# Gate arithmetic and sums of x queued behind the latest weight split, in a fused mLSTM and attention layer

## The chip, the cores and the metric

The kernel runs on one core of a Trainium2 chip. The metric is the device time of one execution in microseconds (us). Five engines work side by side, each with its own queue of instructions: TensorE (PE in the profile; PEld is its loading of weights), VectorE (DVE), ScalarE (ACT), GpSimd (POOL) and SyncE (SP), which here only starts DMA transfers. An engine takes its instructions strictly in the order of its queue: one that waits holds up all behind it.

## The reference

One layer of a decoder is computed for a prompt of 512 tokens and for 8 x 4 sample tokens, 544 tokens together, in float32. What matters here:

```python
u = jnp.einsum('btd,dc->btc', x, w_in)                  # 2048 -> 18952 columns
# q_m, k_m, v_m, o_m, z_m, q_a, k_a, v_a, z_a, g_m, g_a, i_pre, f_pre
ig = i_pre + b_igate                                    # 4 heads: "the gates"
lf = log_sigmoid(f_pre + b_fgate)
b = cumsum(lf)                                          # per chunk, then running maxima, exp: decay factors of the mLSTM
h_m = mlstm(q_m, k_m, v_m, ig, lf);  h_a = sliding_window_attention(q_a, k_a, v_a)
y = sigmoid(g_m) * (branch_m @ w_proj_m) + sigmoid(g_a) * (branch_a @ w_proj_a)
out = layernorm(alpha * x + y @ w_out)
```

The keys and values of the attention (k_a, v_a) and the last state are outputs too.

## The kernel before

**Precision.** Each float32 operand is split into a high part (a rounding copy on ACT) and a low part (the difference, on DVE). `split` (L196 to L202) does it for a block of weights of 128 x 1024: `A.copy(wh)` at L200 and `V.tensor_tensor(wl)` at L201; `hilo` (L239) does it for activations. A product is three matmuls: high x high, high x low, low x high.

**Stage 1, plain products.** x is transposed on TensorE and split (L287 to L310). Then `gemm` computes two blocks of attention values (VA_, L536) and two of keys (KA, L546), each in two halves of the 2048 rows, with TensorE's results in a pair of PSUM banks, of which there are two buffers (`mm`, L216). Beside these there are four small PSUM buffers of one bank (`sm`, L118). Within the second value product stand the matmuls of the gates (`gates_half`, L325 to L343), whose results lie in a third `mm` tile, `gates_ps`.

**Stage 2, pairs.** Pairs of weight blocks are computed from seven half products in place of eight (`paired`, L645). They need sums of quarters of x: `x_sums` (L496) makes `s1`, `n2` and `n3`, `last_sum` (L515) makes `s4`. Before half product number n of a pair `prepare` (L585) forms a sum of weights (L592) and splits it; that is written three half products ahead and has a raised priority (`AHEAD = 400`). `wh` and `wl` have two buffers each, so a split waits until TensorE is done with the half product two before its own. `half_product` (L604) issues 16 matmuls with the high weights (L612) and 8 with the low ones (L614). `gather` (L616) collects results. The first three pairs are the merge gates: at their end `end_gates` (L1163) puts a sigmoid on both results.

**What sets the order.** The text is traced first. A scheduler with a model of the engines' times then orders each engine's queue: of the instructions that are ready it takes the one with the best priority (the place in the text, less what `high_priority` grants), so work can move far ahead of its place. `tc.issue_after(ins)` ties what is traced under it to a place behind `ins` on the same engine; it is an order, not a wait for the end of `ins`. In stage 2 TensorE's queue alone keeps the order of the text (L1216).

**Side work** is written as generators. `spawn` (L136) puts one into the list `live`; `tick` (L141) lets each run to its next `yield`. `products` calls `tick` four times in each plain product of stage 1 (`every=4`), `paired` once after each half product. The generators here are `attn_values` (L466) and `attn_keys` (L482), which turn values and keys to rows with transposes on TensorE; `x_sums`; `gates` (L345), which computes the decay factors in rows of 4 x 544 in several stages and ends with transposes on TensorE (L448 to L462); `attentions` (L794), which waits until the gates have ended; and `samples`. Before, `drain` (L552) runs all generators of stage 1 to their end ahead of stage 2, and the first stage of `gates` is written just ahead of the pairs (L1211).

Of the kernel before, what the change touches and what calls it, by code (L numbers as in the profile page):

```python
# [23 lines left out]
NTS = 4  # L24
# [55 lines left out]
def _build(tc, nc, i, o, es):  # L80
# [43 lines left out]
    def r32(ap):  # L124
        return ap.bitcast(F32)

    def two(ap):
        return ap.rearrange("p (a b) -> p a b", a=2)
# [7 lines left out]
    def spawn(g):  # L136
        live.append(g)
# [8 lines left out]
    def drain():  # L146
        while live:
            tick()
# [47 lines left out]
    def split(raw, p=None, tags=("wh", "wl")):  # L196
        p = p or wp
        wh = p.tile([128, 8, 128], F32R, tag=tags[0], name=nm("wh"))
        wl = p.tile([128, 8, 128], F32R, tag=tags[1], name=nm("wl"))
        A.copy(wh[:], raw[:])  # L200
        V.tensor_tensor(out=wl[:], in0=raw[:], in1=r32(wh[:]), op=ALU.subtract)  # L201
        return wh, wl  # L202

    def products(ps, half, wh, wl, xh, xl, cols, every=8):
        for kk in range(8):
# [10 lines left out]
    def mm():  # L216
        return psA["mm"].tile([128, 2, 512], F32, tag="mm", name=nm("mm"))
# [107 lines left out]
    def gates_half(ps, half):  # L325
        raw = wr.tile([128, 8, 128], F32, tag="raw", name=nm("graw"))
        nc.sync.dma_start(raw[:, :, 0:8], win[:, half * 8:half * 8 + 8, GI:GI + 8])
        wa = wp.tile([128, 8, 128], F32R, tag="wh", name=nm("wga"))
        wb = wp.tile([128, 8, 128], F32R, tag="wl", name=nm("wgb"))
        G.memset(r32(wa[:]), 0.0)  # L330
        G.memset(r32(wb[:]), 0.0)
        for g in range(2):
            src = raw[:, :, g * 4:g * 4 + 4]
            hi = wa[:, :, g * 32:g * 32 + 4]
            A.copy(hi, src)
            A.copy(wb[:, :, g * 32:g * 32 + 4], src)
            V.tensor_tensor(out=wa[:, :, 64 + g * 32:68 + g * 32], in0=src, in1=r32(hi), op=ALU.subtract)
        for kk in range(8):
            k = half * 8 + kk
            for n, (a, b) in enumerate(((wa, xh), (wb, xl))):  # L340
                for f, c, w in EVEN:
                    PE.matmul(ps[:, f, :w], a[:, kk], b(k, c, w),
                              start=(k == 0 and n == 0), stop=(k == 15 and n == 1))  # L343

    def gates(ps):  # L345
# [7 lines left out]
            return ap.unsqueeze(2).to_broadcast([4, NB, NTS])  # L353

        ig, fg, u, u2 = row(), row(), row(), row()
        A.copy(two(u), ps[64:68, :, :272])
        A.copy(two(u2), ps[96:100, :, :272])
        V.scalar_tensor_tensor(two(ig), ps[0:4, :, :272], bi[:, 0:1], two(u), op0=ALU.add, op1=ALU.add)
        V.scalar_tensor_tensor(two(fg), ps[32:36, :, :272], 0.0, two(u2), op0=ALU.add, op1=ALU.add)
        V.tensor_scalar(fg, fg, bi[:, 1:2], None, op0=ALU.add)  # L360
        yield
        e_ = row()
        A.activation(e_, fg, AF.Abs)
        A.activation(e_, e_, AF.Exp, scale=-1.0)
# [101 lines left out]
    def attn_values(kk, vt):  # L466

        yield
        yield
        pt, pt2 = sm(), sm()  # L470
        for b in range(4):
            PE.transpose(pt[:, b * 128:b * 128 + 128], vt[:, b * 128:b * 128 + 128], ident)
        PE.transpose(pt2[:32, 0:128], vt[:, SEQ:T], ident)
        cs = slice(kk * 128, kk * 128 + 128)
        vr, vs = ev(512), ev(128)
        A.copy(vr[:], pt[:])
        V.tensor_copy(vs[:32], pt2[:32, 0:128])
        nc.sync.dma_start(d_vr[0:SEQ, cs].rearrange("(b p) c -> p b c", p=128), blk(vr[:]))
        nc.sync.dma_start(d_vr[SEQ:T, cs], vs[:32])
        nc.sync.dma_start(vb_p[0].rearrange("t k d -> t (k d)")[:, cs], vr[:, 384:512])  # L480
# [15 lines left out]
    def x_sums():  # L496

        for ch in range(4):
            ks_ = slice(ch * 2, ch * 2 + 2)
            r11, r21, r22 = (tx.tile([128, 2, HT], F32, tag="tx", name=nm("tx")) for _ in range(3))  # L500
            G.tensor_tensor(out=r21[:], in0=r32(a21[0][:, ks_]), in1=r32(a21[1][:, ks_]), op=ALU.add)
            k0 = (ch * 2) % 4
            h22, l22 = (r32(xk2[p][ch // 2][:, k0:k0 + 2, HT:T]) for p in range(2))
            V.tensor_tensor(out=r22[:], in0=h22, in1=l22, op=ALU.add)
            G.tensor_tensor(out=r11[:], in0=r32(a11[0][:, ks_]), in1=r32(a11[1][:, ks_]), op=ALU.add)
            V.tensor_tensor(out=r22[:], in0=r22[:], in1=r21[:], op=ALU.subtract)
            hilo(r22[:], s1[0][:, ks_], s1[1][:, ks_])
            yield
            V.scalar_tensor_tensor(r21[:], r11[:], -1.0, r21[:], op0=ALU.mult, op1=ALU.subtract)
            hilo(r21[:], n3[0][:, ks_], n3[1][:, ks_])  # L510
            V.tensor_tensor(out=r11[:], in0=r11[:], in1=r22[:], op=ALU.subtract)
            hilo(r11[:], n2[0][:, ks_], n2[1][:, ks_])
            yield
# [22 lines left out]
    for kk in range(2):  # L536
        ps = gemm(win, VA_ + kk * 128, xh, xl, raws=((raw0[0], raw0[1]), (raw0[2], None))[kk], every=4, prio=150 * kk,
                  before=gates_between if kk else None)
        if kk == 0:
            spawn(x_sums())  # L540
            gates_ps = mm()
        vt = ev()
        with ahead_of_sums():
            A.copy(two(vt[:]), pv(ps))
        spawn(attn_values(kk, vt))
    for kk in range(2):  # L546
        ps = gemm(win, KA + kk * 128, xh, xl, every=4, prio=150)
        kt = ev()
        with ahead_of_sums():
            A.copy(two(kt[:]), pv(ps))  # L550
        spawn(attn_keys(kk, kt))
    drain()  # L552
    for src, dst in ((d_ks, kb_s), (d_vr[SEQ:T], vb_s)):
        nc.sync.dma_start(dst[:, 124:128].rearrange("b t k d -> b t (k d)"), src.rearrange("(b t) c -> b t c", t=NTS))
    nc.sync.dma_start(kb_s[:, 0:124], i["state_attn_k"][:, NTS:128])
    nc.sync.dma_start(vb_s[:, 0:124], i["state_attn_v"][:, NTS:128])

# [236 lines left out]
    def attentions():  # L794
        while gates_ in live:
            yield
        for _ in last:
            pass
        esG.close()
        sp["pz"] = pool(esQ, "pz", 1)  # L800
        open_attention()
        state["open"] = True
        for k in range(16):
            if k % 4 == 0:
                kv = kv_head(k // 4)
            while k not in waiting:
                yield
            for _ in range(2 if k % 4 else 4):
                yield
            yield from attention(k, *waiting.pop(k), kv)  # L810
            state["done"] = k + 1
        esB.close()
        yield from sample_attention()
        esT.close()
        open_samples()
        state["samples"] = True
# [390 lines left out]
        work += part(h)  # L1207
    work += merge_gates[7:]
    last = last_sum(s4)
    gates_ = gates(gates_ps)  # L1210
    next(gates_)  # L1211
    spawn(gates_)
    spawn(attentions())
    spawn(samples())

    with tc.manual_schedule(engines={PE.engine}):  # L1216
# [413 lines left out]
```

## Time and profile before

| | |
|---|---|
| time of 3 runs | 2534.22 us median, 2531.38 to 2538.44 |
| the profiled execution | 2535.28 us, its span from first to last instruction 2533.5 us |
| mean granted TensorE clock | 0.994 |
| busy share of the span | PE 99%, PEld 96%, DVE 67%, ACT 46%, POOL 13% |
| stage 1 and the first pairs | 28 to 130 us of the span |

In rows of the timeline the columns are: start (us), duration (us), engine, line, operation, output <- inputs, shapes, count, and in brackets the idle time of the engine ahead of it with what ended it. A row that merges several instructions gives the time from the first to the last. `L201` is line 201 of the kernel. In rows of stages each engine's busy time is followed by the count of instructions in brackets; then come the granted clock of TensorE, the busy share of the DMA engines and what they moved in GB/s.

### The profile page before, as it was taken

The numbers are of one execution on the slowest core, as the hardware profiler recorded it, in microseconds if no ns is written. First come the engines' busy times: TensorE is split into PE (matmuls) and PEld (weight loads), VectorE is DVE, ScalarE is ACT, GpSimd is POOL, SyncE is SP. The second block draws the span as 40 slices with busy tenths as digits, with TensorE's granted clock in tenths as the row PEclk, the third lists the DMA queues.
The fourth block names the chain that finished last, engine by engine and source line by source line (L and its number), as shares of the span: only waits on it lengthen the run. The fifth ranks groups of instructions, "written<-read, shape, count | busy, mean of one in ns | idle before, by whom it ended". The sixth has DMA issues, their size and how long they took to land.

```text
span 2533.5 us, 48923 instructions
## 1 busy us (share of the span) xinstructions
PE 2504.9 (99%) x19995; PEld 2442.9 (96%) x19995; DVE 1701.5 (67%) x2506; ACT 1174.8 (46%) x1911; POOL 326.0 (13%) x406
## 2 busy tenths in 40 slices
PE   8999999999999999999999999999999999999997
PEld 7999999999999999999999999999999999999997
DVE  7867677677777787588777888877765653333336
ACT  4447667667667665433434344344533332222221
POOL 2111121121121110131111222100000000000002
PEclk9999999999999999999999999999999999999999
DMA  6566666666666654377585785874554555446332
GB/s 192 135 166 153 163 147 158 159 145 161 156 147 160 154 134 131 97 240 242 172 267 174 233 243 149 257 226 127 183 177 164 168 177 157 136 128 193 108 95 85
DMA packets 537104, 421.88 MB, mean 167 GB/s; under 512 B 43536, under 2 KB 449344, under 8 KB 536592
## 3 DMA queue, kind: packets, MB, share of 16 engines
q1 hardware_dynamic: 526800, 382.05, 51.2%
q0 software_dynamic: 10080, 36.70, 8.0%
q8 instruction: 157, 2.57, 0.4%
q14 instruction: 67, 0.55, 0.1%
HBM read 297.67 MB, written 86.42 MB: 152 GB/s over the span
## 4 chain that ended last, share of the span: by engine, by line
PE 93%; DVE 2%; DMA 1%; issue 1%; ACT 0%; DVEq 0%; ACTq 0%
PE bank L612 39%; PE mm L209 21%; PE bank L614 19%; PE sm L1293 2%; PE sum L1104 1%; PE sm L1325 1%; PE sm L1338 1%; PE sm L718 1%; PE sm L758 1%; PE sm L748 1%; PE sm L209 1%; DMA raw<-in_w_in 1%; PE sm L1109 1%; DVE z L1532 0%; PE sm L917 0%
## 5 line engine op out<-in xcount | busy, mean ns | idle before, releaser
L200 ACT CAST wh<-raw 128x1024 fp32r<-128x1024 f32 x604 | 632.6, 1048 | 946.0 <-PE bank L612 540.6
L201 DVE TENSOR_TENSOR wl<-raw,wh 128x1024 fp32r<-128x1024 f32 x604 | 748.5, 1241 | 353.0 <-ACT wh L200 346.4
L612 PE MATMUL bank<-xk,wh 128*128 128x272 f32 x2304 | 315.8, 289 | 0.0
L612 PEld LDWEIGHTS bank<-xk,wh 128*128 128x128 f32 x2304 | 297.8, 188 | 2.8 <-issue 1.5
L592 DVE TENSOR_TENSOR raw<-raw,raw 128x1024 f32<-128x1024 f32 x218 | 277.9, 1275 | 10.1 <-DMA raw<-in_w_in 6.3
L209 PE MATMUL mm<-bh,wl 128*128 128x272 f32 x1024 | 214.4, 289 | 0.0
L209 PE MATMUL mm<-bh,wh 128*128 128x272 f32 x1024 | 214.2, 290 | 0.0
L209 PE MATMUL mm<-bl,wh 128*128 128x272 f32 x1024 | 213.4, 288 | 0.0
L631 POOL TENSOR_TENSOR ev<-p,ev 128x272 f32<-128x272 f32 x72 | 102.3, 1421 | 505.3 <-ACT ev L630 475.6
L614 PE MATMUL bank<-xk,wl 128*128 128x272 f32 x1152 | 167.1, 287 | 0.0
L209 PEld LDWEIGHTS mm<-bh,wh 128*128 128x128 f32 x1024 | 160.5, 188 | 2.3 <-issue 2.3
L209 PEld LDWEIGHTS mm<-bl,wh 128*128 128x128 f32 x1024 | 161.8, 188 | 0.0
L209 PEld LDWEIGHTS mm<-bh,wl 128*128 128x128 f32 x1024 | 160.6, 188 | 0.0
L614 PEld LDWEIGHTS bank<-xk,wl 128*128 128x128 f32 x1152 | 153.5, 188 | 0.0
L612 PE MATMUL bank<-n2h,wh 128*128 128x272 f32 x576 | 149.1, 292 | 2.0 <-ACT wh L200 2.0
L612 PE MATMUL bank<-a11h,wh 128*128 128x272 f32 x576 | 149.5, 291 | 0.0
L612 PE MATMUL bank<-s4h,wh 128*128 128x272 f32 x576 | 148.6, 291 | 0.0
L612 PE MATMUL bank<-s1h,wh 128*128 128x272 f32 x576 | 148.6, 291 | 0.1
L612 PE MATMUL bank<-a11l,wh 128*128 128x272 f32 x576 | 148.5, 290 | 0.0
L612 PE MATMUL bank<-n2l,wh 128*128 128x272 f32 x576 | 148.3, 289 | 0.0
L612 PE MATMUL bank<-n3h,wh 128*128 128x272 f32 x576 | 147.5, 289 | 0.0
L612 PE MATMUL bank<-n3l,wh 128*128 128x272 f32 x576 | 146.9, 288 | 0.0
(433 smaller groups left out, 5407.6 us busy)
## 6 DMA issues: line engine op xcount, KB each, us to landing
raw<-in_w_in SPq DMA_DIRECT2D x296, 512.0 KB
raw<-raw POOLq DMA_DIRECT2D x70, 512.0 KB, 4.9
C<-in_state_mlstm_C SPq DMA_DIRECT2D x32, 1024.0 KB
out<-C SPq DMA_DIRECT2D x64, 512.0 KB
raw<-in_w_proj_a SPq DMA_DIRECT2D x32, 512.0 KB
raw<-in_w_proj_m SPq DMA_DIRECT2D x32, 512.0 KB
raw<-in_w_out SPq DMA_DIRECT2D x32, 512.0 KB
d_sgm<-ev SPq DMA_DIRECT2D x16, 272.0 KB
```

The lines of the kernel that those rows point to most:

```text
L200: A.copy(wh[:], raw[:])
L201: V.tensor_tensor(out=wl[:], in0=raw[:], in1=r32(wh[:]), op=ALU.subtract)
L209: PE.matmul(ps[:, f, :w], a[:, kk], b(k, c, w), start=(k == 0 and n == 0), stop=(k == 15 and n == 2))
L592: V.tensor_tensor(out=w[out][:], in0=w[a][:], in1=w[b][:], op=ALU.add)
L612: PE.matmul(ps, wh[:, k], x(p, k), start=(first and k == 0 and p == 0), stop=False, skip_group_check=True)
L614: PE.matmul(ps, wl[:, k], x(0, k), start=False, stop=(k == 7), skip_group_check=True)
L631: G.tensor_tensor(out=c22, in0=p1, in1=c11, op=ALU.subtract)
L718: PE.matmul(pp[:, c0 + w0:c0 + 256], qs[a][:, j * 128:j * 128 + 128], kx[:, k0:k0 + 256 - w0], start=(n == 0), stop=(n == 1))
L748: PE.transpose(pt[:, (m - m0_) * 128:(m - m0_) * 128 + 128], s_[:, b, 128:256] if own else s_[:, b + 1, 0:128], ident)
L758: PE.matmul(po[:, b * 128:b * 128 + n], VA[:, b], p_[:, 2 * b:2 * b + n // 128], start=(b == 0 and m == 0), stop=(b == 3 and m == 1), skip ...
L1104: PE.matmul(pC[b * 32:b * 32 + 32, :], qz[:, b], ct[:, b], start=(s, c) == (0, 0), stop=not more, tile_position=(0, b * 32))
L1293: PE.matmul(pp[:, 0:258], a[:, b * 128:b * 128 + 128], b_[:, b, f], start=(b == 0 and n == 0), stop=(b == 3 and n == 2))
```

## The change

Four things are changed.

1. `split` remembers the latest copy to `wh` and the latest subtraction to `wl`. A new wrapper `held` runs each stage of a generator under `issue_after` of both, so what the stage puts on ACT is queued behind the latest `wh` copy in the text and what it puts on DVE behind the latest `wl`. `x_sums` and `gates` run in it. `x_sums` yields three times per piece in place of two.
2. `gates_ps` is two small `sm` tiles in place of one `mm` tile, and the first stage of `gates` works on each half of the tokens.
3. The first stage of `gates` is written ahead of the key products. Twelve yields follow it in place of one.
4. The `drain` ahead of stage 2 is gone. Only `x_sums` is run to its end there; the rows of the second key block are made in the first rounds of stage 2, and the DMAs of the last key and value rows follow when both `attn` generators have ended, ahead of `attentions`.

```diff
         wl = p.tile([128, 8, 128], F32R, tag=tags[1], name=nm("wl"))
-        A.copy(wh[:], raw[:])
-        V.tensor_tensor(out=wl[:], in0=raw[:], in1=r32(wh[:]), op=ALU.subtract)
+        state["wh"] = A.copy(wh[:], raw[:])
+        state["wl"] = V.tensor_tensor(out=wl[:], in0=raw[:], in1=r32(wh[:]), op=ALU.subtract)
         return wh, wl
+
+    def held(g):
+
+        while True:
+            with tc.issue_after(state["wh"].ins), tc.issue_after(state["wl"].ins):
+                if next(g, StopIteration) is StopIteration:
+                    return
+            yield
...
         ig, fg, u, u2 = row(), row(), row(), row()
-        A.copy(two(u), ps[64:68, :, :272])
-        A.copy(two(u2), ps[96:100, :, :272])
-        V.scalar_tensor_tensor(two(ig), ps[0:4, :, :272], bi[:, 0:1], two(u), op0=ALU.add, op1=ALU.add)
-        V.scalar_tensor_tensor(two(fg), ps[32:36, :, :272], 0.0, two(u2), op0=ALU.add, op1=ALU.add)
+        for f in range(2):
+            c = slice(f * HT, f * HT + HT)
+            A.copy(u[:, c], ps[f][64:68, :HT])
+            A.copy(u2[:, c], ps[f][96:100, :HT])
+            V.scalar_tensor_tensor(ig[:, c], ps[f][0:4, :HT], bi[:, 0:1], u[:, c], op0=ALU.add, op1=ALU.add)
+            V.scalar_tensor_tensor(fg[:, c], ps[f][32:36, :HT], 0.0, u2[:, c], op0=ALU.add, op1=ALU.add)
         V.tensor_scalar(fg, fg, bi[:, 1:2], None, op0=ALU.add)
-        yield
+        for _ in range(12):
+            yield
...
             G.tensor_tensor(out=r11[:], in0=r32(a11[0][:, ks_]), in1=r32(a11[1][:, ks_]), op=ALU.add)
+            yield
             V.tensor_tensor(out=r22[:], in0=r22[:], in1=r21[:], op=ALU.subtract)
...
         if kk == 0:
-            spawn(x_sums())
-            gates_ps = mm()
+            sums = held(x_sums())
+            spawn(sums)
+            gates_ps = sm(), sm()
...
+    gates_ = held(gates(gates_ps))
+    next(gates_)
     for kk in range(2):
         ps = gemm(win, KA + kk * 128, xh, xl, every=4, prio=150)
...
-    drain()
-    for src, dst in ((d_ks, kb_s), (d_vr[SEQ:T], vb_s)):
-        nc.sync.dma_start(dst[:, 124:128].rearrange("b t k d -> b t (k d)"), src.rearrange("(b t) c -> b t c", t=NTS))
+    while sums in live:
+        tick()
...
-    gates_ = gates(gates_ps)
-    next(gates_)
     spawn(gates_)
-    spawn(attentions())
+
+    def then_attentions():
+
+        while any(g.__name__ in ("attn_values", "attn_keys") for g in live):
+            yield
+        for src, dst in ((d_ks, kb_s), (d_vr[SEQ:T], vb_s)):
+            nc.sync.dma_start(dst[:, 124:128].rearrange("b t k d -> b t (k d)"), src.rearrange("(b t) c -> b t c", t=NTS))
+        yield from attentions()
+
+    spawn(then_attentions())
```

In `gates_half` the matmuls write `ps[f][:, :w]` in place of `ps[:, f, :w]`.

More of the change, by code (lines that the diff above doesn't have):

```diff
@@ L341, in gates_half @@
                 for f, c, w in EVEN:
-                    PE.matmul(ps[:, f, :w], a[:, kk], b(k, c, w),
+                    PE.matmul(ps[f][:, :w], a[:, kk], b(k, c, w),
                               start=(k == 0 and n == 0), stop=(k == 15 and n == 1))
```

## The prediction

> **What bounds the kernel now.** I read the first part of the page, then a table of the span by stage, then TensorE's timeline where it is not full.
>
> ```profile
> PE 2504.9 (99%) x19995; PEld 2442.9 (96%) x19995; DVE 1701.5 (67%) x2506; ACT 1174.8 (46%) x1911; POOL 326.0 (13%) x406
> ```
>
> Stages (start:end, length, busy us and instructions of PE, PEld, DVE, ACT, POOL, granted clock, DMA share, GB/s):
>
> ```profile
> 0.00:28.00 28.00, 22.32 (x148) 20.15 (x149) 11.19 (x24) 11.90 (x28) 4.78 (x9) 0.94 0.83 231
> 28.00:130.00 102.00, 93.49 (x712) 91.48 (x711) 89.68 (x141) 47.35 (x74) 19.30 (x21) 0.97 0.58 150
> 130.00:2480.00 2350.00, 2349.68 (x18816) 2292.09 (x18815) 1568.54 (x2297) 1110.40 (x1801) 286.37 (x367) 1.00 0.60 168
> ```
>
> TensorE (PE) bounds. From 130 to 2480 us it idles 0.3 us; the change touches nothing before 28 or in the tail. Everything to be won lies in 28 to 130 us: 8.5 us idle and a clock of 0.97. VectorE (DVE) is busy 88% there. The idle pieces, each with its releaser:
>
> ```profile
> 30.02 0.66 PE L300 MATMUL sm<-cc,t 128*128 128x128 f32 x4 [1.01 <-DVE xk L241]
> 42.85 0.39 PE L209 MATMUL mm<-a11h,wh 128*128 128x272 f32 x1 [2.36 <-ACT ev L544]
> 56.88 0.52 PE L209 MATMUL mm<-xk,wl 128*128 128x272 f32 x2 [1.13 <-DVE wl L201]
> 88.99 0.33 PE L487 MATMUL sm<-cc,ev 128*128 128x128 f32 x1 [1.44 <-ACT ev L550]
> 118.79 0.39 PE L612 MATMUL bank<-n2h,wh 128*128 128x272 f32 x1 [1.97 <-ACT wh L200]
> ```
>
> Two of them are followed by a slow clock (last columns but two: 0.53 and 0.57):
>
> ```profile
> 44.30:47.90 3.60, 3.60 (x19) 3.60 (x18) 3.56 (x5) 0.00 (x0) 2.86 (x2) 0.53 0.65 166
> 119.40:123.40 4.00, 4.00 (x22) 4.00 (x21) 1.73 (x2) 1.73 (x3) 0.86 (x1) 0.57 0.67 161
> ```
>
> That costs (1-0.53) x 3.6 = 1.7 and (1-0.57) x 4.0 = 1.7 us.
>
> **Part 1, sums of x behind the splits: a gain.** In before the sums (tile tx) stand ahead of weight splits that TensorE waits for. Around 40 us:
>
> ```profile
> 38.27 1.05 ACT L200 CAST wh<-raw 128x1024 fp32r<-128x1024 f32 x1 [3.21 <-PE mm L342]
> 42.20 0.60 ACT L544 COPY ev<-mm 128x544 f32<-128x544 f32 x1
> ...
> 38.52 1.50 DVE L506 TENSOR_TENSOR tx<-tx,tx 128x544 f32<-128x544 f32 x1
> 41.53 1.22 DVE L201 TENSOR_TENSOR wl<-raw,wh 128x1024 fp32r<-128x1024 f32 x1
> ```
>
> The high half was ready at 39.3, but DVE came to the low half at 41.53, after three sum operations, and the eviction L544 queued on ACT behind the casts of sums. After the change every sum is traced inside the second value product, so it is held behind that split: the low half ends near 40.6, about when TensorE gets there. The two small gate banks leave both large PSUM buffers to the value products, so the matmul no longer waits for L544 either. Bounds 0 to 2.36 + 1.7 = 4.1; I take 3.6, as the split still ends a little late. At 30.02 the rows of x queue in the same way behind sums: 0 to 1.0, I take 0.7. At 56.88 (wh cast below ends at 53.7, wl only at 55.61 after three fillers) I take 1.1 of 0 to 1.1:
>
> ```profile
> 52.64 1.05 ACT L200 CAST wh<-raw 128x1024 fp32r<-128x1024 f32 x1 [1.25 <-PE mm L342]
> ...
> 53.71 0.71 DVE L506 TENSOR_TENSOR tx<-tx,tx 128x544 f32<-128x544 f32 x1
> 55.61 1.21 DVE L201 TENSOR_TENSOR wl<-raw,wh 128x1024 fp32r<-128x1024 f32 x1
> ```
>
> Cover: the held sums (by the code 7 DVE operations in each of 4 pieces, 28 x 0.71 = 20 us) now run between about 41 and 88 us, one piece's third behind each split; six splits of 1.2 us stand there and, with the gate arithmetic gone, DVE has the room. Without that cover the second and third half product of the first pair, which read them, would wait.
>
> The gate rows in two small banks cost four copies and four additions of half the width for two and two: some tenths of a us on ACT and DVE, behind the last value split, under TensorE's key product. They hold two of the four small buffers that the rows of x are also turned in; at worst TensorE waits there for what it waits for at 30.02, 1.0. I take 0, since the last of those transposes came before the first gate matmul:
>
> ```profile
> 32.52 0.60 PE L300 MATMUL sm<-cc,t 128*128 128x128 f32 x4
> 34.25 0.36 PE L342 MATMUL mm<-a11h,wga 128*128 128x272 f32 x1
> ```
>
> **Part 2, keys' rows behind the first pair: nothing.** The transposes no longer stand ahead of the first pair, but the first bank is laid over the closed large buffers and, as I read the code, waits for the same eviction L550. Bounds: gain 0 to 1.44; I take 0. The last rows' two DMAs move behind these transposes on SP's queue:
>
> ```profile
> 91.15 0.38 SPq L494 DMA_DIRECT2D d_ks<-ev  x1
> 95.63 0.67 SPq L554 DMA_DIRECT2D out<-d_ks  x1
> 100.95 1.46 SPq L193 DMA_DIRECT2D raw<-in_w_in  x2
> ```
>
> L554 waits for d_ks to land, 4.1 us, and SP's queue with it. Behind the second half product that wait ends some 6 us later, about where the next pair's weight loads are issued at 100.95, so these may be 0.7 us late (L554's own issue). The cast that needs them ran at 110.56 and ended at 111.6; its half product, the ninth, begins 24 us after the first, which follows the transposes of 88.99 at about 89.2, so at 113.2. The 1.6 us between hide it: 0.
>
> **Part 3, gate arithmetic out of the first pairs: a gain.** ACT before the wait at 118.79:
>
> ```profile
> 110.56 1.05 ACT L200 CAST wh<-raw 128x1024 fp32r<-128x1024 f32 x1 [0.83 <-DVE raw L592]
> 111.63 1.28 ACT L1166 ACT_TABLE_LOAD   x1
> 112.92 0.66 ACT L1166 ACTIVATE ev<-ev 128x544 f32<-128x544 f32 x1
> 113.60 1.28 ACT L425 ACT_TABLE_LOAD   x1
> 114.89 0.66 ACT L425 ACTIVATE t<-t 4x544 f32<-4x544 f32 x1
> 115.57 1.28 ACT L1166 ACT_TABLE_LOAD   x1
> 116.86 0.66 ACT L1166 ACTIVATE ev<-ev 128x544 f32<-128x544 f32 x1
> 117.70 1.98 ACT L200 CAST wh<-raw 128x1024 fp32r<-128x1024 f32 x2
> ```
>
> The gates' exponential between two sigmoids costs two more table loads, 3.2 us, and the cast comes late. Later, the first pair's sigmoids stand alone, the cast runs near 114.5, and the wait and its slow clock go: 0 to 1.97 + 1.7 = 3.7; I take 3.7.
>
> The Trainium skill speaks against these clock terms ("TensorE: Matmul & The Clock Gate", section "HAM oscillation — how this bites in real kernels"): it asks only for no idle gaps over about 3.4 us. The trace disagrees: gaps of 1.97 and 2.36 us were followed by 0.57 and 0.53. By the rule the gain would be 3.4 us smaller.
>
> **Part 4, where the gates now arrive: a loss.** This decides. Each round of the waiting generators follows one half product. Before, the arithmetic began in round 1 and its transposes (L448 to L462), whose place on TensorE is fixed by the text, stood in round 10:
>
> ```profile
> 122.06 1.53 PE L614 MATMUL bank<-n2h,wl 128*128 128x272 f32 x8
> 123.42 0.60 PE L448 MATMUL sm<-cc,t 128*128 128x128 f32 x4
> ...
> 62.04 0.66 ACT L363 ACTIVATE t<-t 4x544 f32<-4x544 f32 x1 [3.57 <-DVE t L360]
> ```
>
> But it ran from 62 us, 27 us ahead of the first half product, hoisted into free places: 61 us from first exponential to transposes. Twelve yields instead of one make these rounds 12 and 21, and the hold forbids the hoisting: what is traced in round 12 stands on its engine behind the split of half product 13 (from 0). That split waits for a buffer, that is for TensorE:
>
> ```profile
> 129.34 2.00 PE bank L612 x16
> 131.34 1.00 PE bank L614 x8
> ...
> 149.55 1.05 ACT L200 CAST wh<-raw 128x1024 fp32r<-128x1024 f32 x1 [1.95 <-PE bank L612]
> 150.63 1.23 DVE L201 TENSOR_TENSOR wl<-raw,wh 128x1024 fp32r<-128x1024 f32 x1 [1.51 <-ACT wh L200]
> ```
>
> A half product takes 3.0 us. With S the start of the first, the cast of 13 follows the 16 matmuls of 11: S+35. Then 1.05 + 0.66 + 1.28 (table) + 0.66 gives the exponential at S+38.7. DVE's part is traced a round later, behind the low split of 14, which follows the end of 12: S+39 + 1.2 = S+40.2. TensorE reaches the transposes after half product 20: S+63. That leaves 22.8 us. What DVE must do in it, and what it has free (the gates' tile t alone after the first exponential; a whole pair of steady work, 7 half products):
>
> ```profile
> 66.00:120.00 54.00, 0.00 (x0) 0.00 (x0) 21.27 (x40) 1.75 (x4) 0.68 (x3) 0.99 0.53 132
> ...
> 147.50:168.53 21.03, 21.03 (x171) 21.03 (x170) 12.42 (x13) 9.72 (x13) 3.13 (x3) 1.00 0.73 177
> ```
>
> Steady work leaves (21.03-12.42)/21.03 = 41% free, 9.3 of the 22.8 us; splits carry a higher priority than gates. Left at S+63: 21.27 - 9.3 = 12.0. Add the last exponential with its table load, 1.9, and one more split in the stand, 1.2; take off 1.6, about what the splits can be late unnoticed: TensorE stands 13.5 us. Below: if all gate work went ahead and only the six splits 15 to 20 shared DVE, 21.27 + 6 x 1.23 - 22.8 = 5.9. Above: if scattered gaps give only a fourth of the 22.8, 21.3 - 5.7 + 1.9 = 17.5. A slow clock follows a gap, 1.7 by the rows above. What is queued behind the standing transposes is all TensorE work; the attention that opens after the gates is needed only from round 28, so it isn't late.
>
> **Sum.** Gains 3.6 + 0.7 + 1.1 + 0 + 3.7 = 9.1 (0 to 11.3 with the 1.44). Loss 13.5 + 1.7 = 15.2 (7.6 to 19.2). Net +6.1 on the profiled execution's 2535.28, its span of 2533.5 and 1.8 around it: 2541.4. That execution is 1.1 above the median of 2534.22, so 2540.3 for the median.
>
> **Rivals.**
> Faster: the gates are ready in time, and only the gains remain, 2535.3 - 9.1 - 1.1 = 2525.1. For it: in before DVE packed gates and splits tightly up to 116 us with no wait. Against: the chain alone, 21.27 + 1.9 us, fills the 22.8 with no split at all.
> Slower: the gates give way to every split and gather and the stand at the transposes is the long one, 17.5: +17.5 + 1.7 - 9.1 = +10.1, 2544.3. It decides from a stand of 15.0 on (9.1 + 7.6 - 1.7). For it: gate operations come as one dependent chain, each of which can miss a gap. Against: TensorE's stand itself stops new splits.
> The hold does not do what it says: the waits before 130 us pass to another releaser (L550 took its place once already at 88.99, and the weight DMA stands close behind), half the gain is lost, 15.2 - 4.5 = +10.7, 2544.9. Against: the rows name DVE and ACT order each time.
>
> **How the numbers follow.** A measurement of this kernel tells about 0.3%, 7.6 us, from no change. Forecast (net -1 to +7.5) 46%, faster 17%, the long stand 22%, gains halved 15%. The likeliest's own range is 2533 to 2542. Taking in both slower rivals and the edge of the faster one: 2526 to 2549. Faster by over 0.3%: 0.15, as a part of that rival stops short; slower: 0.37; the same: 0.48.
>
> **What would show it.** Right: one TensorE wait of 10 to 16 us at L448, released by DVE or ACT, near 145 us, and no waits at 42.85, 56.88 and 118.79; VectorE's L369 after 120 us. Wrong: no wait at L448, or gate arithmetic on DVE before the second pair has ended, or new waits at L612 for s1 or n2.

## The result and the profile after

The changed kernel takes 2551.75 us (median, 2545.36 to 2553.11); the kernel before, run beside it, takes 2532.34. The ratio is 1.0065, with a 95% interval of 1.0054 to 1.0077: **slower by some 16.5 us** (0.0065 x 2534.22; the ratio is that of the means, the medians are 19.4 us apart). The forecast was 2540.3, about 6 us slower, and its range ended at 2549. The sign was right and the size was not.

Line numbers are shifted by the change: those of the paired stage are 14 higher than before (L626 and L628 are the half product's matmuls, L606 the sum of weights), the gates' and the sums' lines 11 higher (L380 the reciprocal, L436 the last exponential, L459 to L473 the transposes), and those of `gemm` and `hilo` 8 higher (L217, L248, L249). The keys' eviction is L565 (L550 before).

First the stages of the profiled execution (its time 2545.36 us, its span 2543.6), with the columns of the stage rows before:

```profile
28.00:130.00 102.00, 96.62 (x759) 95.87 (x758) 76.35 (x101) 49.01 (x70) 22.56 (x16) 0.98 0.61 157
130.00:200.00 70.00, 55.07 (x409) 54.30 (x409) 52.70 (x82) 29.26 (x40) 8.85 (x13) 0.85 0.51 123
```

Up to 130 us TensorE now idles 5.4 us where it idled 8.5. Then, where it had hardly idled at all, it idles 14.9 us in 70, at a clock of 0.85. The idle pieces, from TensorE's timeline of the changed kernel:

```profile
68.37 0.40 PE L217 MATMUL mm<-a11h,wl 128*128 128x272 f32 x1 [0.46 <-DVE wl L201]
75.93 0.52 PE L217 MATMUL mm<-xk,wl 128*128 128x272 f32 x2 [1.27 <-DVE wl L201]
85.61 0.60 PE L626 MATMUL bank<-a11h,wh 128*128 128x272 f32 x1 [3.66 <-ACT ev L565]
134.69 1.28 PE L628 MATMUL bank<-s1h,wl 128*128 128x272 f32 x8 [0.21 <-DVE wl L201]
165.70 1.09 PE L459 MATMUL sm<-cc,t 128*128 128x128 f32 x4 [14.72 <-ACT t L436]
```

The waits at 30.02, 42.85, 56.88 and 118.79 are gone. In place of 1.44 us at the first bank stand 3.66, and the stand at the gates' transposes is 14.72. Two of these gaps are followed by a slow clock (granted clock: last column but two):

```profile
85.50:89.50 4.00, 3.89 (x20) 3.90 (x21) 4.00 (x7) 0.25 (x2) 0.00 (x0) 0.61 0.26 81
166.00:170.00 4.00, 4.00 (x20) 3.67 (x18) 1.04 (x7) 0.73 (x2) 0.00 (x0) 0.50 0.02 4
170.00:174.00 4.00, 4.00 (x19) 3.97 (x18) 0.25 (x2) 0.34 (x1) 0.00 (x0) 0.51 0.37 98
```

That costs 0.39 x 4 = 1.6 us behind the first bank and 0.50 x 4 + 0.49 x 4 = 4.0 behind the stand.

**The gates' chain after**, from ScalarE's and VectorE's timelines, its first and last steps and the slowest single one:

```profile
124.13 1.28 ACT L375 ACT_TABLE_LOAD   x1
125.42 0.66 ACT L375 ACTIVATE t<-t 4x544 f32<-4x544 f32 x1
...
162.44 1.28 ACT L435 ACT_TABLE_LOAD   x1 [9.22 <-DVE t L408]
...
164.90 0.65 ACT L436 ACTIVATE t<-t 4x544 f32<-4x544 f32 x1
```

```profile
128.19 0.42 DVE L379 TENSOR_SCALAR t<-t 4x544 f32<-4x544 f32 x1
...
129.68 3.53 DVE L380 RECIPROCAL t<-t 4x544 f32<-4x544 f32 x1
...
161.66 0.70 DVE L408 TENSOR_TENSOR t<-t,t 4x544 f32<-4x544 f32 x1
```

And VectorE's time while TensorE was still at work ahead of the transposes, first all of it, then that on the gates' tile `t` alone:

```profile
128.00:151.00 23.00, 22.93 (x27) 1.00 0.68 162
...
128.00:151.00 23.00, 12.28 (x13) 1.00 0.68 162
151.00:164.00 13.00, 9.57 (x24) 0.60 0.49 124
```

VectorE was full. The gates had 12.28 of 23 us, more than half, and still 9.57 us of their own work were left when TensorE arrived.

**What the hold does to VectorE early on.** Rows of VectorE in the changed kernel, behind them the stage of both kernels from 28 to 50 us:

```profile
36.34 1.23 DVE L201 TENSOR_TENSOR wl<-raw,wh 128x1024 fp32r<-128x1024 f32 x1 [3.52 <-ACT wh L200]
...
48.19 1.23 DVE L201 TENSOR_TENSOR wl<-raw,wh 128x1024 fp32r<-128x1024 f32 x1 [7.58 <-PE sm L350]
```

```profile
28.00:50.00 22.00, 22.00 (x180) 21.95 (x179) 10.15 (x17) 8.29 (x16) 4.04 (x4) 1.00 0.69 208
```

```profile
28.00:50.00 22.00, 18.43 (x131) 17.62 (x130) 21.17 (x32) 9.41 (x22) 8.99 (x8) 0.92 0.71 203
```

The first of the two stage rows is after, the second before. A split waits for what releases its buffers, that is for TensorE; whatever is queued behind it waits too. So VectorE, which had worked 21.17 of these 22 us, works 10.15. TensorE is full there now, which was the point, but 11 us of VectorE's work are pushed toward the pairs, where VectorE is the scarce engine.

**A landmark.** The first matmul of the sample attention comes long after all that the change touches. First before, then after (shortest, median and longest duration in ns, then start of the first and the last):

```profile
L871 PE MATMUL sm<-kT,qas x64: 269/270/293, 953.2 to 967.2; 64*32 64x128 f32 x64
```

```profile
L885 PE MATMUL sm<-kT,qas x64: 269/270/293, 966.2 to 980.2; 64*32 64x128 f32 x64
```

It comes 13.0 us later. The idle pieces give 5.4 - 8.5 + 14.9 = +11.8 and the slow clocks 1.6 + 4.0 - 3.4 = +2.2 (the 3.4 are the two of before). Together that is 14.0, 1 us more than the landmark shows.

### The profile page after: what moved, and what is told of

Same layout as the page of the kernel before. It is cut to its first block, busy times and chain, and to the rows that moved or that the text cites. A ratio compares the mean times of both kernels' runs of the same rounds, so it can differ in the third digit from the quotient of the medians.

```text
span 2543.6 us, 48933 instructions
## 1 busy us (share of the span) xinstructions
PE 2503.1 (98%) x19995; PEld 2442.1 (96%) x19995; DVE 1703.0 (67%) x2508; ACT 1177.9 (46%) x1915; POOL 330.1 (13%) x406
## 4 chain that ended last, share of the span: by engine, by line
PE 91%; DVE 2%; DMA 1%; issue 0%; ACT 0%; DVEq 0%; ACTq 0%
PE bank L626 38%; PE mm L217 21%; PE bank L628 19%; PE sm L1314 2%; PE sum L1118 1%; PE sm L1346 1%; PE sm L1359 1%; PE sm L732 1%; PE sm L772 1%; PE sm L762 1%; PE sm L217 1%; DMA raw<-in_w_in 1%; PE sm L1123 1%; DVE z L1553 0%; PE sm L931 0%
## 5 line engine op out<-in xcount | busy, mean ns | idle before, releaser
L626 PE MATMUL bank<-xk,wh 128*128 128x272 f32 x2304 | 315.7, 289 | 0.0
L626 PEld LDWEIGHTS bank<-xk,wh 128*128 128x128 f32 x2304 | 297.8, 188 | 2.7 <-issue 1.5
L606 DVE TENSOR_TENSOR raw<-raw,raw 128x1024 f32<-128x1024 f32 x218 | 278.0, 1275 | 11.2 <-DMA raw<-in_w_in 7.1
L217 PE MATMUL mm<-bh,wl 128*128 128x272 f32 x1024 | 214.4, 289 | 0.0
L217 PE MATMUL mm<-bh,wh 128*128 128x272 f32 x1024 | 214.2, 290 | 0.0
L217 PE MATMUL mm<-bl,wh 128*128 128x272 f32 x1024 | 213.4, 288 | 0.0
L628 PE MATMUL bank<-xk,wl 128*128 128x272 f32 x1152 | 167.1, 287 | 0.0
L217 PEld LDWEIGHTS mm<-bh,wh 128*128 128x128 f32 x1024 | 160.5, 188 | 2.3 <-issue 2.3
L217 PEld LDWEIGHTS mm<-bl,wh 128*128 128x128 f32 x1024 | 161.8, 188 | 0.0
L217 PEld LDWEIGHTS mm<-bh,wl 128*128 128x128 f32 x1024 | 160.6, 188 | 0.0
L626 PE MATMUL bank<-a11h,wh 128*128 128x272 f32 x576 | 151.6, 294 | 3.7 <-ACT ev L565 3.7
L628 PEld LDWEIGHTS bank<-xk,wl 128*128 128x128 f32 x1152 | 153.5, 188 | 0.0
L626 PE MATMUL bank<-a11l,wh 128*128 128x272 f32 x576 | 150.3, 293 | 0.0
L626 PE MATMUL bank<-s4h,wh 128*128 128x272 f32 x576 | 148.6, 291 | 0.0
L626 PE MATMUL bank<-s1h,wh 128*128 128x272 f32 x576 | 148.6, 291 | 0.1
L626 PE MATMUL bank<-n3h,wh 128*128 128x272 f32 x576 | 147.5, 289 | 0.0
L626 PE MATMUL bank<-n2h,wh 128*128 128x272 f32 x576 | 147.4, 289 | 0.0
L626 PE MATMUL bank<-n3l,wh 128*128 128x272 f32 x576 | 146.9, 288 | 0.0
L626 PE MATMUL bank<-s4l,wh 128*128 128x272 f32 x576 | 146.7, 287 | 0.0
```

Source lines behind the costliest of these rows:

```text
L217: PE.matmul(ps[:, f, :w], a[:, kk], b(k, c, w), start=(k == 0 and n == 0), stop=(k == 15 and n == 2))
L606: V.tensor_tensor(out=w[out][:], in0=w[a][:], in1=w[b][:], op=ALU.add)
L626: PE.matmul(ps, wh[:, k], x(p, k), start=(first and k == 0 and p == 0), stop=False, skip_group_check=True)
L628: PE.matmul(ps, wl[:, k], x(0, k), start=False, stop=(k == 7), skip_group_check=True)
```

## The experiments

In each, all results of the reference are still computed. The shift of the landmark against before (953.2) stands beside each time, since it is free of what happens later in the span. It is read from one profile of each kernel.

### The gates not held

```diff
-    gates_ = held(gates(gates_ps))
+    gates_ = gates(gates_ps)
```

> The changed kernel, but the gates are not held behind the splits (the sums of x still are); the transposes of the gates stay in round 21. Theory (the hold takes from the gate arithmetic the free places before the pairs, and TensorE stands 14.7 us at the transposes for it): the arithmetic runs again from about 55 us, no stand at the transposes, no slow clock behind it; only waits below 4 us are left in the first 130 us, and the time is 2525 to 2531 us against 2532 before and 2552 changed. Rival 1 (the later round itself, not the hold, makes the arithmetic late): a stand of 10 us or more stays and the time is above 2545. Rival 2 (the loss lies in other parts, such as the wait of 3.7 us at the first bank): the stand goes, but the time stays above 2540.

Measured: 2547.35 us, ratio 1.0046 (1.0031 to 1.0061); landmark 962.9, +9.7. The stand is gone, but other waits have taken its place:

```profile
PE bank L626 <- DVE s4l L249: 4.9, 2, 3.5
PE bank L626 <- DVE n2l L249: 4.2, 1, 4.2
PE bank L626 <- ACT s4h L248: 1.8, 1, 1.8
PE bank L626 <- DVE s1l L249: 1.8, 1, 1.8
```

(us in total, times, longest.) TensorE waits for the sums of x themselves, now late. From 60 to 120 us VectorE is busy 59.9 us of 60 in this run, and 21.6 of them go to the gates' tile `t`: the free gates run into the time in which VectorE must catch up on the held sums. So the expectation of a gain falls: freeing one of the two moves the shortage instead of ending it.

### The transposes four rounds later

```diff
-        for _ in range(4):
+        for _ in range(8):
             yield
         for src, rep, dst, m in
```

> The changed kernel with eight in place of four rounds between the last exponentials of the gates and their transposes, so TensorE reaches them four half products (12 us) later, in round 25; nothing else differs. Theory (VectorE's share: while TensorE works, splits take 59% of VectorE, so 12 us more of work give the gates only 0.41 x 12 = 4.9 us): the stand shrinks from 14.7 to about 9.8 us, and the time by about 5 us, to 2541 to 2548. Rival (the gates are a chain of fixed length, and every us that TensorE comes later is a us less of standing): the stand shrinks by 12 to about 2.7 us, and the time falls by 12 us or more, to 2533 to 2540.

Measured: 2537.96 us, ratio 1.0014 (1.0001 to 1.0028); landmark 958.3, +5.1.

```profile
170.62 1.09 PE L459 MATMUL sm<-cc,t 128*128 128x128 f32 x4 [7.11 <-ACT t L436]
```

TensorE arrived at 170.62 - 7.11 = 163.5 in place of 151.0, 12.5 us later, and the gates ended 4.9 us later, so the stand shrank by 7.6. Neither extreme holds: not all 12.5 are won, and the gates have more of them than the 41% that the prediction took from steady work. 4.9 us is what four splits of 1.23 take, and VectorE's rows from 128 us to the end of the gates say the same: 13 splits stand there in place of 9, with 4.8 us more of work, and the sums of weights and the gathers beside them are as many as before. So in this place each further half product took one split from the gates and left them the rest.

### The gates held, but started early

```diff
-        for _ in range(12):
-            yield
+        yield
         e_ = row()
...
+        for _ in range(12):
             yield
         A.activation(T2[0:4], mrow, AF.Exp, scale=-1.0)
```

The twelve yields now stand ahead of the last exponentials, so the chain begins in round 1 and its transposes stay in round 21.

> The changed kernel, held as it is, but the gate arithmetic starts in round 1 in place of round 12, and the eleven rounds are waited ahead of the last exponentials, so these stay in round 17 and the transposes in round 21. Theory (what is late is the start, 11 half products or 33 us): VectorE has 33 us more, of which 41% are 13.5 us, about the stand; the stand shrinks to 0 to 2 us, and the time is 2527 to 2535. Rival 1 (holding behind splits costs in itself, since each stage must wait for a split that waits for TensorE): the stand stays above 8 us and the time above 2543. Rival 2 (the exponential early among the sigmoids brings back the table loads): the stand goes but a wait of about 2 us of L626 for a wh cast comes back before 130 us, and the time is 2532 to 2537.

Measured: 2532.26 us, ratio 0.9989 (0.9977 to 1.0001); landmark 951.9, -1.3. The waits of more than 1 us from 28 to 200 us:

```profile
PE bank L626 <- ACT ev L565: 3.6, 1, 3.6
PE mm L217 <- DVE wl L201: 1.8, 2, 1.3
PE sm L460 <- DVE ev L448: 1.5, 1, 1.5
```

No stand, and none of the late sums either, with the same hold. So the loss of the change lies in where its twelve yields stand: with the chain started eleven rounds sooner the ratio is 0.9989 in place of 1.0065.

### TensorE kept busy in the stand

```diff
+        pw = sm()
+        for _ in range(110):
+            PE.transpose(pw[:, 0:128], ident, ident)
         for src, rep, dst, m in
```

The 110 transposes are added work whose result nothing reads.

> The changed kernel with 110 transposes of the identity, whose results nobody reads, ahead of the gates' transposes; they add some 12 to 14 us of TensorE work in the place where it stood idle. Theory (the idle time is followed by a slow clock, 8.2 us at 0.5 in the profiled run and longer in the others, whose clock over the whole run is 0.989 in place of 0.992): TensorE is busy in the stand, the wait left at the gates' transposes is 0 to 3 us, the granted clock stays at 1.00 behind it, and the time falls by 4 to 10 us, to 2541 to 2547, with a narrower spread. Rival (the slow clock and the spread of the runs come from elsewhere): the time stays at 2548 to 2553 or rises by the added work.

Measured: 2551.95 us, ratio 1.0056 (1.0037 to 1.0074); landmark 965.7, +12.5. What is left of the stand, and the stages behind it:

```profile
165.94 0.63 PE L462 MATMUL sm<-cc,t 128*128 128x128 f32 x4 [2.69 <-ACT t L436]
```

```profile
166.00:170.00 4.00, 4.00 (x24) 3.80 (x25) 1.45 (x11) 0.72 (x2) 0.00 (x0) 0.66 0.00 0
170.00:174.00 4.00, 4.00 (x19) 4.00 (x19) 0.00 (x0) 0.89 (x1) 0.00 (x0) 0.50 0.41 102
```

A gap of 2.69 us brings a slow clock that costs 0.34 x 4 + 0.50 x 4 = 3.4 us, nearly the 4.0 that follow a gap of 14.72. Between these two the cost hardly grows with the gap. Through the 12 us of transposes themselves the clock stayed at 1.00. Whether a stand without any gap would keep the clock up wasn't reached here.

### The sums held, nothing else

The kernel before, with `held`, the extra yield in `x_sums`, and

```diff
-            spawn(x_sums())
+            spawn(held(x_sums()))
```

> The kernel before with one part of the change alone: the sums of x are held behind the latest split and yield three times per piece. Gates, keys and banks are as before. Theory now (VectorE is the scarce engine from 28 us to about 165 us; the hold leaves it idle between 28 and 50 us, and some 11 us of sums come later, beside the gate arithmetic, which is not held): the waits at 42.85 and 56.88 shrink, but L612 waits for s1, n2 or s4 for 8 to 16 us in total, and the time is 2539 to 2549 against 2532 to 2537 before. Rival (the prediction's part 1: the hold on the sums is a gain of its own): the waits before 60 us go, none above 3 us comes, and the time is 2526 to 2533.

Measured: 2545.03 us, ratio 1.0042 (1.0029 to 1.0054); landmark 962.6, +9.4. Its waits (the half product's matmuls stand at L621 here):

```profile
PE bank L621 <- DVE s4l L249: 3.4, 3, 2.5
PE bank L621 <- ACT s4h L248: 3.3, 1, 3.3
PE bank L621 <- DVE n2l L249: 2.8, 1, 2.8
PE bank L621 <- DVE s1l L249: 2.0, 1, 2.0
```

Holding the sums (with the extra yield) and nothing else is a loss of 11 us: the sums are late for the half products that read them. This is the picture of the first experiment, with the gates in their old place.

### The gates held, the sums not

```diff
-            sums = held(x_sums())
+            sums = x_sums()
```

> The changed kernel, but the sums of x are not held; the gates are, from round 12 on, as in the change. Theory (the stand at the transposes is set by what VectorE can do of the gates between half product 12 and half product 21, whatever came before): the stand stays at 12 to 16 us and the time at 2543 to 2553. Rival (the sums pushed behind make the gates late): VectorE is ahead by 11 us, the stand is below 8 us and the time below 2541.

Measured: 2549.70 us, ratio 1.0062 (1.0048 to 1.0075); landmark 967.4, +14.2. From its waits:

```profile
PE sm L459 <- ACT t L436: 14.7, 1, 14.7
...
PE bank L626 <- ACT ev L565: 1.4, 1, 1.4
```

The stand is the same to the tenth. So it doesn't come from the sums. And the first bank's wait is 1.4 here, as before the change: its growth to 3.7 comes with the held sums.

### Early gates, sums not held

The edits of the third and the sixth experiment together.

> As the changed kernel with the held gates started in round 1, but with the sums of x not held. Theory (VectorE fills 28 to 50 us again, and the gates, held behind the splits, come behind the sums): no wait above 3 us for s1, n2 or s4 and none above 2 us at the gates' transposes; the waits of before at 42.85 and 56.88 us are partly back; the time is 2527 to 2535. If the hold on the sums is worth something when the gates are early, this is slower than the 2532 of the run that held both; if it costs, it is faster.

Measured: 2535.88 us, ratio 1.0003 (0.9995 to 1.0012); landmark 949.3, -3.9. From 28 to 200 us no wait is longer than 1.8 us. By the landmark it is the best of all, and yet the time is that of before; the section on the hardware comes back to this. What the hold on the sums does early on shows here too: without it TensorE waits 1.80 us for a low split at 41.61 (1.79 at 41.93 in the experiment before), where the changed kernel doesn't wait.

### Two waits of the early version mended

The third experiment's kernel, with its last sums held too, and a row of the gates' transposes in another buffer (the wait at L460):

```diff
-    last = last_sum(s4)
+    last = held(last_sum(s4))
...
-            rep = ev(128) if len(reps) < 2 else t5(n=128)
+            rep = ev(128) if not reps else t5(n=128) if len(reps) == 2 else tx.tile([128, 2, HT], F32, tag="tx", name=nm("tx"))[:, 0, 0:128]
```

> The changed kernel with the held gates started in round 1, with two more edits: the last sum (s4) is held too, and the second of the two small row copies lies in a tile of the sums in place of one shared with the pairs' results. Theory (the wait of 3.6 us at the first bank comes since ACT stands at a cast of s4 that waits for VectorE, with the eviction L565 behind it; the wait of 1.5 us at the transposes comes from the shared tile): the first falls to 0.5 to 1.5 us and no slow clock follows, the second goes, and the time is 2524 to 2530, below both kernels. Rival (the closing of the large buffers sets the wait at the first bank, whatever ACT does): that wait stays at 3 us or more and the time at 2529 to 2533.

Measured: 2538.82 us, ratio 1.0023 (1.0014 to 1.0032); landmark 958.5, +5.3. Both waits went as meant (the first bank waits 1.4, L460 no more), and dearer ones came:

```profile
104.89 0.59 PE L626 MATMUL bank<-s4l,wh 128*128 128x272 f32 x1 [4.18 <-DVE s4l L249]
108.31 0.59 PE L626 MATMUL bank<-s4h,wh 128*128 128x272 f32 x1 [2.38 <-ACT s4h L248]
111.31 0.59 PE L626 MATMUL bank<-s4l,wh 128*128 128x272 f32 x1 [2.41 <-DVE s4l L249]
```

Held once more, `s4` is too late. The expectation falls.

### The keys' eviction ahead of the cast of `s4`

What makes the first bank wait 3.66 us in the changed kernel can be read from ScalarE's timeline around it, and VectorE's:

```profile
83.45 0.65 ACT L248 CAST s4h<-tx 128x544 fp32r<-128x544 f32 x1 [3.49 <-DVE tx L536]
84.00 1.04 ACT L200 CAST wh<-raw 128x1024 fp32r<-128x1024 f32 x1
84.95 0.60 ACT L565 COPY ev<-mm 128x544 f32<-128x544 f32 x1
```

```profile
82.65 0.71 DVE L536 TENSOR_TENSOR tx<-tx,tx 128x544 f32<-128x544 f32 x1
```

The first cast of `s4h` was queued ahead of a weight cast and of the eviction. It waits for a sum on VectorE that the held sums have made late, and the eviction stands behind it. The test puts the last sums behind the keys' eviction on ScalarE and leaves VectorE alone:

```diff
-            A.copy(two(kt[:]), pv(ps))
+            state["kt"] = A.copy(two(kt[:]), pv(ps))
...
-    last = last_sum(s4)
+    def behind_keys(g):
+        while True:
+            with tc.issue_after(state["kt"].ins):
+                if next(g, StopIteration) is StopIteration:
+                    return
+            yield
+
+    last = behind_keys(last_sum(s4))
```

> The changed kernel with one order altered: s4's sums are queued behind the keys' eviction on ScalarE, so the first cast of s4h, which came at 83.45 after 3.49 us of waiting for VectorE, no longer stands ahead of that eviction (84.95). Theory (that cast made the first bank's wait 3.7 in place of 1.4): the wait at L626 near 85 us falls to about 1.4, and the slow clock of 85 to 89 us (0.55 and 0.60, 1.7 us) goes with it; the stand of 14.7 stays; 2 to 4 us below the changed kernel. Rival (VectorE is what is short, whatever ScalarE's order): the first wait falls, but TensorE waits 2 to 9 us for s4h or s4l some 20 us later, as in the run with the held last sums, and the time is that of the changed kernel or above.

Measured: 2548.92 us, ratio 1.0051 (1.0037 to 1.0064); landmark 963.9, 2.3 us ahead of the changed kernel's.

```profile
29.63 0.66 PE L308 MATMUL sm<-cc,t 128*128 128x128 f32 x4 [2.03 <-DVE xk L249]
...
84.66 0.39 PE L626 MATMUL bank<-a11h,wh 128*128 128x272 f32 x1 [1.45 <-ACT ev L565]
```

```profile
85.00:89.00 4.00, 4.00 (x34) 4.00 (x33) 4.00 (x5) 1.40 (x2) 0.00 (x0) 1.00 0.29 93
```

The wait fell from 3.66 to 1.45 and the clock behind it is full, as the theory has it: 2.2 + 1.6 = 3.8 us. The stand stayed 14.7, and no wait for `s4` came. The 2.03 us at 29.63 are another matter: there VectorE stood 4.69 us at `nsinkb` (L327), for the transfer of the small input `attn_sinks`, and began at 28.64 (in the changed kernel's profile it stood 2.04 us there and began at 27.20); the subtraction for x is queued behind it. Nothing that this edit moves stands there. The gates' first matmul came at 32.51 in place of 31.23, 1.28 us behind, and the landmark is 2.3 ahead: 3.6 us were won between the two, close to the 3.8.

### The same in the early version

The edits of the third experiment and of the last one together.

> The same order of the eviction in the kernel whose gates start early and stay held (2532.26, ratio 0.9989, first wait 3.6). Theory: without the first wait's excess of 2.2 us and the slow clock behind it 2528 to 2531, ratio 0.997 to 0.9985, no wait of s4. Rival (VectorE short): waits of 2 to 9 us for s4, ratio 0.999 to 1.002.

Measured: 2531.84 us, ratio 0.9991 (0.9982 to 1.0000); landmark 951.7, -1.5: no better than without it.

```profile
101.56 0.37 PE L626 MATMUL bank<-n3h,wh 128*128 128x272 f32 x1 [3.91 <-DVE ev L647]
```

```profile
97.58 3.53 DVE L379 RECIPROCAL t<-t 4x544 f32<-4x544 f32 x1
101.05 0.37 DVE L647 SCALAR_TENSOR_TENSOR ev<-bank,p 128x272 f32<-128x272 f32 x1
```

The gates' reciprocal came before the eviction that a bank was waiting for, and held it 3.5 us. Neither form of the expectation names this wait, but it is of the rival's kind: VectorE is full, and what one operation no longer delays, another does.

## Why the prediction was wrong in size

**Part 1, sums behind the splits.** The waits at 42.85 with its slow clock, at 30.02 and at 56.88 are gone: 2.36 + 1.7 + 1.01 + 1.13 = 6.2. Two waits for low splits in the key products came, 0.46 and 1.27. The net gain is 4.5, and 5.4 had been taken. At 42.85 it took both edits: with the small banks alone a wait of 1.79 for the low split stays (the gates held, the sums not), and with the hold alone one of 0.70 for the eviction (the sums held, nothing else). At 30.02 the prediction had the cause wrong. In the kernel before, VectorE's row ahead of what TensorE waited for is

```profile
28.55 0.83 DVE L319 TENSOR_SCALAR nsinkb<-sinkb 128x32 f32<-128x32 f32 x1 [2.91 <-DMA sinkb<-in_attn_sinks]
```

VectorE stood 2.91 us for the transfer of the small input `attn_sinks`, and of the sums only one (0.74) stood between it and the subtraction for x. The wait comes back with the sums held (1.02 in the sums held only, 2.03 in the eviction ahead) and with the sums free (0.9 in the early gates with free sums). So that the hold removed this 1.01 isn't shown; its absence from the changed kernel's profile may be luck. The step "with the gate arithmetic gone, DVE has the room" held only as long as the gates stayed away. With them in place the same hold lost 11 us (sums held, nothing else). The prediction had named that cover and not its price.

**Part 2, keys' rows: the first step that failed.** That the first bank "waits for the same eviction L550" was right, and the price of nothing was not. That eviction (now L565) came late behind a cast for the held sums: 3.66 in place of 1.44 and 1.6 of slow clock, a loss of 3.8, where the bounds ran from no gain to a gain of 1.44. The order of the eviction alone brings 2.2 and 1.6 of it back (the eviction ahead).

**Part 3, gate arithmetic out of the first pairs.** The wait at 118.79 and its slow clock went: 1.97 + 1.7 = 3.7, as taken.

**Part 4, the loss.** Its mechanism held step by step: one stand at the transposes, released by ScalarE. The pairs begin with 85.61 as S. The exponential was due to end at S + 38.7 = 124.3 and ended at 126.1 (125.42 + 0.66); VectorE's part was due at 125.8 and came at 128.19, TensorE's arrival at 148.6 and came at 151.0. All are some 2 us late, so the 22.8 us between the last two held. The stand came to 14.72 where 13.5 was forecast, inside 5.9 to 17.5, but its terms missed on both sides, and that they nearly cancelled is luck. The gates got 12.28 us of VectorE where 9.3 had been taken. Against that, two operations on weights and a gather (1.20 + 1.21 + 0.42 = 2.8 us) ran in the stand where one split of 1.2 had been taken; the last exponentials took 3.1 us (162.44 to 165.55) in place of 1.9, since two smaller ones stand ahead of the last, L436; and nothing came off for splits that are late unnoticed, where 1.6 had been taken. **The slow clock behind it was the term that was mis-sized**: 4.0 us, and 1.7 had been taken from gaps of 2 us.

**Sum.** Gains of 4.5 + 3.7 and 0.3 (the small wait inside the old transposes) less 3.8 are 4.7, where 9.1 were taken. The loss is 14.7 + 4.0 = 18.7, where 15.2 were. That is +14.0, as the idle pieces and clocks give, and not +6.1. Of the 8 us between, 3.8 are Part 2, 3.5 the stand and its clock, and 0.9 the new waits for low splits, less the 0.3.

From 13.0 at the landmark to about 16.5 in the ratio some 3.5 us are left. These parts don't explain them: the two profiled executions are only 10.1 us apart (2545.36 and 2535.28), and the other four of the changed kernel were slower, at a lower mean clock; see below.

**The rivals.** The faster one (gates in time) needs an earlier start, and with it the time is that of before at best (0.9989), since the hold's gains and its losses then nearly cancel. The long stand was put at 17.5 with the gains kept; what came was the forecast's stand with half the gains. That the waits pass to another releaser, the third rival, is what happened at the first bank, "L550" by name. It had been put at 15% beside the likeliest and not added to it.

**What would show it.** A wait of 10 to 16 us at the transposes: 14.72, but at 165.70, as the wait's end, and not near 145. The reciprocal after 120 us: 129.68. No new waits for `s1` or `n2` in the changed kernel: none, but two kinds in the first experiment.

## What to carry to other kernels

To queue work behind the latest weight split keeps that split early, and it chains the work to whatever the split waits for, here TensorE itself: VectorE lost 11 us out of 22 before the stretch in which it was needed most. Before moving a chain of dependent steps, put its length, and what its engine has free, against the place where the matmul engine's order is fixed; where the chain doesn't fit, start it sooner rather than let it through faster. And when a wait is removed, price the operation that will stand ahead of the next one in that engine's queue: an edit "at nothing" beside a changed queue has a loss among its bounds.

## What the runs showed of the hardware

**The slow clock after a gap.** Gaps of 2.69 (TensorE kept busy), 3.66 and 14.72 us were all followed by a stretch of 4 us, or two, with a mean clock of 0.50 to 0.66. Gaps of 1.45 us weren't followed by it, and one of 2.03 wasn't either (29.63 in the run with the eviction ahead, among the transposes of x; the clock in its stage row is 1.00):

```profile
28.00:32.00 4.00, 2.37 (x20) 2.37 (x21) 3.13 (x8) 1.07 (x2) 0.94 (x1) 1.00 0.63 142
```

Before, gaps of 1.97 and 2.36 were. In the run with the gates held and the sums not, a gap of 1.79 was (0.50 from 44 to 46 us), and one of 1.67 wasn't. So near 2 us it comes in some cases and not in others. The rule of the Trainium skill ("TensorE: Matmul & The Clock Gate", section "HAM oscillation — how this bites in real kernels") asks for no idle gaps above about 3.4 us. By these rows keeping to it isn't enough: a gap of 2.69 cost 3.4 us.

**A switch of tables on ScalarE** cost one table load: 124.13 to 125.42, 1.29 us, with nothing added ahead of the exponential.

**A varying clock far behind the change.** The landmark and the time agree in nearly all kernels (shift in us; the ratio less 1, times 2534):

| kernel | landmark | time |
|---|---|---|
| changed kernel | +13.0 | +16.5 |
| gates not held | +9.7 | +11.7 |
| transposes later | +5.1 | +3.5 |
| held, early | -1.3 | -2.8 |
| busy in the stand | +12.5 | +14.2 |
| sums held only | +9.4 | +10.6 |
| gates held, sums not | +14.2 | +15.7 |
| early, sums not held | -3.9 | +0.8 |
| two waits mended | +5.3 | +5.8 |
| eviction ahead | +10.7 | +12.9 |
| early, eviction ahead | -1.5 | -2.3 |

The differences reach 5 us, and no edit reaches the code behind the landmark. One stretch there has a different clock in each profile, the one of the sample attention's small matmuls. First the run with the transposes later, then the early one with the eviction ahead:

```profile
940.00:1100.00 160.00, 159.89 (x1386) 153.48 (x1385) 116.27 (x159) 78.12 (x127) 29.52 (x33) 1.00 0.50 134
```

```profile
940.00:1100.00 160.00, 159.92 (x1315) 152.96 (x1314) 107.02 (x150) 73.13 (x122) 28.78 (x31) 0.94 0.48 129
```

A clock of 0.94 costs 0.06 x 160 = 9.6 us there. The spans agree: from the landmark to the end it is 1575.6 us in the first (2533.9 - 958.3) and 1585.1 in the second (2536.8 - 951.7), 9.5 more.

The clock over the whole span varies from one execution of a kernel to the next, and the time with it. The early kernel with the eviction ahead took 2529.33 to 2538.57 us in twelve executions, at a mean clock of 0.996 for the fastest and 0.992 for the slowest, and the profiled one is the slowest. Of the changed kernel's five the profiled one, at 0.992, is the fastest; three at 0.989 took 2551.75 to 2553.11, and 0.003 x 2545 is 7.6 us. So its last 3.5 us come with a lower clock in those executions; in which stretch they had it no profile shows. The kernel that is earliest at the landmark had a clock of 0.96 from 940 to 1110 us in its profile, and 1581.6 us from the landmark to the end. What sets the clock in this stretch wasn't tried, nor whether it also follows from the kernel.

None of the versions is clearly faster than the kernel before: the best two, 0.9989 (0.9977 to 1.0001) and 0.9991 (0.9982 to 1.0000), are at its time.
